# Second feed-forward entry: scaling and split by token halves, late factors tied behind direct evacuations, weight sums on VectorE

## The chip, the cores and the metric

The kernel runs on one core of a Trainium2 chip. The time is device microseconds of one execution. The engines are TensorE (PE, matmuls; PEld is its weight load), VectorE (DVE), ScalarE (ACT), GpSimd (POOL) and SyncE (SP, which issues DMAs). Each takes its instructions in a fixed order.

## What is computed

One inference step of a decoder of two layers, for a prompt of 512 tokens and a sample group of 8 tokens that share the weights. The width D is 1024, the feed-forward width 4096. Everything is float32. Cut to what matters:

```python
def rmsnorm(x, g):
    xf = x.astype(F32)
    y = xf * lax.rsqrt(jnp.mean(xf * xf, axis=-1, keepdims=True) + EPS)
    return (y * g.astype(F32)).astype(x.dtype)

def sq_relu_mlp(x, g, w_up, w_down):
    h = rmsnorm(x, g) @ w_up
    return jnp.square(jax.nn.relu(h)) @ w_down

def retention_layer(x, mem_k, mem_v, s0, g_mix, w_in, w_out, g_mlp, w_up, w_down):
    ...
    x = x + jnp.concatenate([o_ret, o_mem], axis=-1) @ w_out
    return x + sq_relu_mlp(x, g_mlp, w_up, w_down), s_new

def window_layer(x, k_ctx, v_ctx, decode, mem_k, mem_v, sinks, g_mix, w_in, w_out, g_mlp, w_up, w_down):
    ...
    x = x + jnp.concatenate([o_swa, o_mem], axis=-1) @ w_out
    return x + sq_relu_mlp(x, g_mlp, w_up, w_down)
```

The trunk is the retention layer, the window layer, and a last rmsnorm.

## The kernel before

The 512 + 8 tokens stand together as 520 columns (`TT`), features on the partitions, so the stream `x` is 8 tiles (`KT`) of 128 features x 520 tokens. `HALVES` are tokens 0 to 255 and 256 to 519, which gives products of 256 and 264 columns. Each float32 operand is split into a high and a low part: ACT casts the high part, DVE subtracts it for the low part. A product of two such operands is three matmuls for each tile: high weight with high and with low activation, low weight with high activation (`product`, L233).

The program has four phases, one after the other: A (retention layer), FA (`mlp(0, False)`, its feed-forward part), B (window layer), FB (`mlp(1, True)`). Each phase has a tile pool of its own, and the pools use the same memory in turn, so a first tile of a phase waits until the tile of the phase before that lay there was read for the last time.

**`mlp`.** The feed-forward width is cut into 4 groups of 8 blocks of 128. `up(g)` makes the 8 blocks of a group, `down(g)` multiplies them into the stream; `ORDER_F` says in which order steps of `up(g)` and `down(g-1)` follow one another, in rounds of one `up` pair and two `down` blocks. In group 0 the first four blocks are direct products, `u100` to `u103` in FB (`u000` to `u003` in FA). The other pairs of blocks go through `seven`: a product of two blocks by seven smaller ones (as in Strassen's method), for which the activations are combined into seven factors, `op[1]` to `op[7]`, and the weights into four sums (`total`, L320), whose engines the string `ENG_W` gives, by pairs of blocks in turn. A `seven` is 84 matmuls on PE (L298); its evacuations are L333 to L349, then L831 and L832.

**`operands`** makes what the entry of a feed-forward phase needs. For each of the 8 tiles, in the order 0, 4, 1, 5, 2, 6, 3, 7 (`BY_PAIR`), it scales `x` by a gain and the factor of the norm before (`f1xg`, L276), splits the result for the direct products (`direct.put`, the low part `hid` of L178), adds the squares of `x` for the norm (`norm.add`: ACT squares, L378, and DVE adds to `f1acc`, L382), and makes the factors from pairs of tiles: four combinations (L264) and seven splits (the low part is L253) for each pair, 11 DVE instructions. The direct products need only the split; the factors are needed from `u104` on.

**The norm.** `m.finish` sums `f1acc` over the partitions on PE (`f1ms`, L392), makes the inverse root by a chain of small DVE steps (L394 to L363, ending in `ry`), spreads it over the partitions (`f1mt`, L409) and copies it on ACT (`f1r`, L413). Only then can the first direct blocks be evacuated (L823). PE's banks for the products are few: three `mm`, two `ws`, two `wt`, one `ot`. Raw weights, high parts and low parts have three buffers each.

The end of phase B is its output projection: the products `ob`, of operands `obh` and `obl` that are split from `wo` (ACT L177, DVE L178), and the residuals `xs` (L440).

The source says what depends on what; the order on each engine is set by the framework's scheduler when the program is built.

Of the kernel before, what the change touches and what calls it, by code (L numbers as in the profile page):

```python
# [16 lines left out]
ALU = mybir.AluOpType  # L17
# [14 lines left out]
FFG = 4  # L32
FK = 8
DIRECT = 2
UK = KT // 2
BY_PAIR = [kt + i * UK for kt in range(UK) for i in range(2)]
EPS = 1e-6
# [7 lines left out]
ROLE_U = ('mm', 'mm', 'mm', 'ws')  # L45
ORDER_F = "uddudduddudd"
ENG_UL = "vvvvvvvv"
ENG_R = dict(a='ppppvppv', m='pppppppv', f='vvvvvvvv', b='vvvvvpvv', y='vppppppv')
ENG_B = "pvvvvvvv"
ENG_W = "pvppppvp"  # L50
BUFS_W = dict(wr=3, wh=3, wl=3)
BUFS_A = dict(blk=2, qkv=6, wp=2, mp=4, wpT=3, qw=1, kvs=1, ld=5)
BANKS = dict(mm=3, ws=2, wt=2, ot=1)
# [62 lines left out]
def build(tc, d, o):  # L116
    nc = tc.nc
    with ExitStack() as ctx:
# [20 lines left out]
        def half(name, dt=F32, shape=None):  # L139
            return hp.tile(shape or [P, 4, TT], dt, name=name, tag="half")  # L140

        def blk(name, shape=None, tag="blk", dt=F32):
            return now["w"].tile(shape or [P, TT], dt, name=name, tag=tag, bufs=now["tags"][tag])
# [11 lines left out]
        f = lambda ap: ap.bitcast(F32)  # L155
        v2 = lambda ap: ap.rearrange("p (a b) -> p a b", a=2)

        class Pair:
# [25 lines left out]
        x = [xs[:, kt, :] for kt in range(KT)]  # L184
# [14 lines left out]
        def gain(name, kt):  # L199
            return gains[:, GAINS.index(name), kt:kt + 1]  # L200
# [45 lines left out]
            nc.vector.scalar_tensor_tensor(  # L246
                out=a.lo(kt), in0=x[kt], scalar=gain(g, kt), in1=f(a.hi(kt)), op0=ALU.mult, op1=ALU.subtract)

        def cut(op, j, src, eng):

            h, l = op[:, 0, j, :], op[:, 1, j, :]
            nc.scalar.copy(out=h, in_=src)
            eng.tensor_sub(out=l, in0=src, in1=f(h))  # L253

        def operands(name, g, scale, direct, norm):

            op, first = {}, {}
            left, right = slice(0, EVEN), slice(EVEN, TT)  # L260

            def combine(i, j, x0, x1, alu):
                t = blk(f"{name}t{i}{j}", [P, EVEN], "t")
                nc.vector.tensor_tensor(out=t, in0=x0, in1=x1, op=alu)  # L264
                put(i, j, t)
                return t

            def put(i, j, src):
                if i not in op:
                    op[i] = half(f"{name}{i}", F32R, [P, 2, UK, EVEN])  # L270
                cut(op[i], j, src, nc.vector)

            for n, kt in enumerate(BY_PAIR):
                j = kt % UK
                y = blk(f"{name}xg{kt}", tag="u")
                nc.vector.scalar_tensor_tensor(out=y, in0=x[kt], scalar=gain(g, kt), in1=scale, op0=ALU.mult, op1=ALU.mult)  # L276
                direct.put(kt, y)
                norm.add(n, x[kt])
                if kt < UK:
                    first[j] = y  # L280
                    put(1, j, y[:, left])
                    combine(5, j, y[:, right], y[:, left], ALU.subtract)
                else:
                    b11, b12, b21, b22 = first[j][:, left], first[j][:, right], y[:, left], y[:, right]
                    t = combine(7, j, b22, b12, ALU.subtract)
                    t = combine(6, j, t, b11, ALU.add)
                    put(3, j, b22)
                    combine(4, j, b21, t, ALU.subtract)
                    put(2, j, b21)
            return op  # L290

        def times(t, w, op, more=False):

# [7 lines left out]
        def seven(src, op, u, name, turn):  # L301


            n = UK * P
            raw = [wp.tile([P, KT * P], F32, name=f"{name}r{i}", tag="wr", bufs=BUFS_W["wr"]) for i in range(2)]
# [62 lines left out]
        class Rms:  # L368
# [6 lines left out]
            def add(self, kt, src):  # L375
# [120 lines left out]
            yield  # L496


        def side_by_side(*pairs):


            last = None
            for pair in pairs:
                for m in reversed(pair):
                    i = m()  # L505
                    if last is not None:
                        tc.add_manual_dep(i.ins, last.ins.name, mybir.DependencyInfo(
                            mybir.DependencyClass.NoSync, mybir.DependencyReason.DATA), reason="side by side")
                    last = i

        def mem_attention(l, qm, out):
# [281 lines left out]
        def mlp(l, last):  # L793
            before, scale = now["norm"]
# [4 lines left out]
            def room(name, odd):  # L799
                t = Pair(name)  # L800
                if odd:
                    t.t.update({(part, i): high[:, 2 * j + i] for j, part in enumerate("hl") for i in range(2)})
                return t

            hids = [room(f"hid{l}{g}", g % 2) for g in range(FFG)]
            xg = room(f"xg{l}", True)
            m = Rms(TT, TT // 5, f"f{l}", "blk")
            op = operands(f"f{l}", f"mlp{l}", scale, xg, m)
            r = []

            def up(g, hid):

                n0 = 2 * DIRECT if g == 0 else 0
                for n in range(n0):
                    w = weights(d["w_up"][l, g * FK + n], D, f"u{l}{g}{n}")
                    t = [part(f"u{l}{g}{n}", s, ROLE_U[(2 * n + s) % len(ROLE_U)]) for s in range(2)]
                    for s in range(2):
                        product(t[s], w, xg, 0, s, BY_PAIR, 1, BY_PAIR)
                    if not r:
                        r.append(m.finish(before)[1])  # L820
                    u = blk(f"u{l}{g}{n}", tag="u")
                    for s, ts in enumerate(HALVES):
                        nc.vector.scalar_tensor_tensor(out=u[:, ts], in0=t[s], scalar=0.0, in1=r[0][:, ts], op0=ALU.max, op1=ALU.mult)  # L823
                    nc.scalar.square(out=u, in_=u)
                    hid.put(n, u)
                    yield
                for n in range(n0, FK, 2):
                    u = [blk(f"u{l}{g}{n}{i}", tag="u") for i in range(2)]
                    seven([d["w_up"][l, g * FK + n + i] for i in range(2)], op, u, f"u{l}{g}{n}", n // 2)
                    for i in range(2):  # L830
                        nc.vector.scalar_tensor_tensor(out=u[i], in0=u[i], scalar=0.0, in1=r[0], op0=ALU.max, op1=ALU.mult)  # L831
                        nc.scalar.square(out=u[i], in_=u[i])  # L832
                        hid.put(n + i, u[i])
                    yield
# [280 lines left out]
```

## Time and profile before

| | us |
|---|---|
| median of 3 runs | 1238.98 |
| lowest and highest | 1237.83, 1239.64 |
| profiled execution | 1237.81 |
| its span | 1236.0 |
| DVE busy | 833.5 |
| ACT busy | 534.1 |
| POOL busy | 221.3 |

The span goes from the first to the last instruction of the profiled execution; its time includes 1.8 us more around it. The mean granted clock of TensorE was 0.983 of its full speed.

### The profile page before, as it was taken

The numbers are of one execution on the slowest core, as the hardware profiler recorded it, in microseconds if no ns is written. First come the engines' busy times: TensorE is split into PE (matmuls) and PEld (weight loads), VectorE is DVE, ScalarE is ACT, GpSimd is POOL, SyncE is SP. The second block draws the span as 40 slices with busy tenths as digits, with TensorE's granted clock in tenths as the row PEclk, the third lists the DMA queues.
The fourth block names the chain that finished last, engine by engine and source line by source line (L and its number), as shares of the span: only waits on it lengthen the run. The fifth ranks groups of instructions, "written<-read, shape, count | busy, mean of one in ns | idle before, by whom it ended". The sixth has DMA issues, their size and how long they took to land. (4 is left out here: it accounts for less than half of the span.)

```text
span 1236.0 us, 23670 instructions
## 1 busy us (share of the span) xinstructions
PE 1198.1 (97%) x9718; PEld 1140.1 (92%) x9718; DVE 833.5 (67%) x1616; ACT 534.1 (43%) x997; POOL 221.3 (18%) x196
## 2 busy tenths in 40 slices
PE   8999999999999999999999998899799999999996
PEld 7999989999999999999999786579799999999996
DVE  7676777789766666675557658558786576666634
ACT  6232442354554444444324326455464444444532
POOL 2301100001312112121024114110232121121110
PEclk9999999999999999999999998889799999999998
DMA  8345622222223232232324354001122232322412
GB/s 308 108 150 174 213 77 72 88 86 72 75 94 120 86 120 87 101 103 77 122 94 143 105 165 145 27 1 54 49 100 105 77 113 86 119 87 95 142 38 69
DMA packets 43724, 128.25 MB, mean 104 GB/s; under 512 B 5048, under 2 KB 10304, under 8 KB 43488
## 3 DMA queue, kind: packets, MB, share of 16 engines
q1 hardware_dynamic: 41376, 119.79, 28.1%
q0 software_dynamic: 2240, 6.95, 1.6%
q8 instruction: 76, 1.25, 0.4%
q14 instruction: 32, 0.26, 0.1%
HBM read 117.65 MB, written 9.08 MB: 103 GB/s over the span
## 5 line engine op out<-in xcount | busy, mean ns | idle before, releaser
L440 DVE TENSOR_TENSOR xs<-d,xs 128x264 f32<-128x264 f32 (+1 forms) x128 | 53.9, 422 | 102.2 <-PE d L233 102.2
L233 PE MATMUL d<-hid,dw 128*128 128x256 f32 (+1 forms) x384 | 46.9, 283 | 0.0
L233 PEld LDWEIGHTS d<-hid,dw 128*128 128x128 f32 x384 | 46.3, 188 | 0.1
L832 ACT ACTIVATE u<-u 128x520 f32<-128x520 f32 x56 | 35.6, 636 | 21.9 <-DVE u L831 21.9
L641 POOL DMA_DIRECT2D out_ret_s<-s x12 | 6.8, 569 | 135.5 <-DVE s L640 102.8
L702 ACT ACTIVATE wp<-wp,wnm 128x256 f32<-128x256 f32 (+1 forms) x48 | 22.5, 471 | 13.3 <-DVE wes L699 9.4
L233 PE MATMUL ob<-obh,obw 128*128 128x256 f32 (+1 forms) x128 | 26.8, 297 | 0.9 <-ACT obh L177 0.7
L707 POOL TENSOR_SCALAR wp<-wp,wsm 128x256 f32<-128x256 f32 (+1 forms) x32 | 15.4, 496 | 53.7 <-ACT wp L702 27.3
L233 PEld LDWEIGHTS ob<-obh,obw 128*128 128x128 f32 x128 | 21.3, 197 | 3.3 <-ACT obh L177 1.7
L178 DVE TENSOR_TENSOR hid<-u,hid 128x520 fp32r<-128x520 f32 x32 | 23.2, 726 | 0.0
L831 DVE SCALAR_TENSOR_TENSOR u<-u,f1r 128x520 f32<-128x520 f32 x28 | 22.7, 811 | 0.4
L831 DVE SCALAR_TENSOR_TENSOR u<-u,f0r 128x520 f32<-128x520 f32 x28 | 22.7, 811 | 0.4
L526 ACT ACTIVATE p<-ms,nm 128x256 f32<-128x256 f32 x32 | 14.8, 475 | 18.5 <-DVE nm L524 16.8
L715 PEld LDWEIGHTS wt<-c,wp 128*128 128x128 f32 x84 | 10.4, 154 | 12.9 <-POOL wp L707 7.2
L715 PE MATMUL wt<-c,wp 128*128 128x128 f32 x84 | 16.4, 312 | 5.1 <-POOL wp L707 2.7
L177 ACT CAST hid<-u 128x520 fp32r<-128x520 f32 x32 | 20.1, 628 | 1.0
L233 PE MATMUL ob<-obl,obw 128*128 128x256 f32 (+1 forms) x64 | 18.4, 300 | 1.6 <-DVE obl L178 1.6
L178 DVE TENSOR_TENSOR obl<-wo,obh 128x128 fp32r<-128x128 f32 x24 | 6.9, 288 | 17.5 <-ACT obh L177 17.5
L505 PE MATMUL ws<-kvb,qb 64*128 64x256 f32 (+1 forms) x96 | 16.6, 433 | 1.3 <-DVE wp L692 0.6
L524 DVE TENSOR_REDUCE nm<-ms 128x2 f32<-128x512 f32 x16 | 10.3, 685 | 10.1 <-PE ms L505 10.1
L717 ACT COPY wpT<-wt 128x384 f32<-128x384 f32 x28 | 12.8, 479 | 8.6 <-PE wt L715 8.0
L692 DVE SCALAR_TENSOR_TENSOR wp<-cb,ws 128x256 f32<-128x256 f32 (+1 forms) x48 | 15.4, 375 | 0.1
(1996 smaller groups left out, 5115.1 us busy)
## 6 DMA issues: line engine op xcount, KB each, us to landing
kc<-in_mem_k SPq DMA_DIRECT2D x16, 256.0 KB, 4.3
vc<-in_mem_v SPq DMA_DIRECT2D x16, 256.0 KB, 4.6
s<-in_S SPq DMA_DIRECT2D x12, 256.0 KB, 5.2
out_ret_s<-s POOLq DMA_DIRECT2D x12, 256.0 KB, 2.6
xs<-in_xT SPq DMA_DIRECT2D x8, 260.0 KB, 4.3
out_yT<-xs SPq DMA_DIRECT2D x2, 528.0 KB, 3.2
memx<-in_memT SPq DMA_DIRECT2D x1, 1024.0 KB, 9.0
u004r<-in_w_up SPq DMA_DIRECT2D x2, 512.0 KB, 3.2
```

What stands on the lines that cost most here:

```text
L177: nc.scalar.copy(out=self.hi(kt, sl, rows), in_=src)
L178: eng.tensor_sub(out=self.lo(kt, sl, rows), in0=src, in1=f(self.hi(kt, sl, rows)))
L233: nc.tensor.matmul(t, w[:, ws], a(kt, HALVES[s]), start=kt == k[0] and m == 0, stop=kt == k[-1] and m == 2)
L440: nc.vector.tensor_add(out=x[mb][:, ts], in0=t, in1=x[mb][:, ts])
L505: i = m()
L526: nc.scalar.activation(out=t[:, b, :], in_=s[hh][:, b, :], func=AF.Exp, bias=nm[:, b:b + 1], accum_out=sm[:, b:b + 1])
L692: nc.vector.scalar_tensor_tensor(out=pv[:, j, :], in0=cb["nd"][:, k0:], scalar=float(SLOPES[6 * kb + j]), in1=sv[j // 3][j % 3], op0=ALU.m ...
L702: nc.scalar.activation(out=pv[:, j, :], in_=pv[:, j, :], func=AF.Exp, bias=nm[:, j:j + 1], accum_out=sm[:, j:j + 1])
L707: (nc.gpsimd if j % 3 in POOL_N else nc.vector).tensor_scalar(out=pv[:, j, :], in0=pv[:, j, :], scalar1=sm[:, j:j + 1], scalar2=1.0, op0=A ...
L715: nc.tensor.transpose(t[:, i * P:i * P + P], p[:, 3 * hh + i, kk * P:kk * P + P], ident)
L831: nc.vector.scalar_tensor_tensor(out=u[i], in0=u[i], scalar=0.0, in1=r[0], op0=ALU.max, op1=ALU.mult)
L832: nc.scalar.square(out=u[i], in_=u[i])
```

## The change

There are four parts.

- Late factors: the factors of the first two pairs of tiles are made at once, those of the last two (`LATE = 2`) only in `up(0)`, behind the first and the second direct block. Each DVE instruction of these is tied by an order dependence (`behind`) to come after the block's second evacuation; the casts on ACT aren't tied. This holds for both feed-forward phases.
- Halves: in FB alone, the scaling and the split for the direct products are done for tokens 0 to 255 and for 256 to 519 apart.
- Weight sums: all four sums of each `seven` are on DVE. In the program 84 of them were on POOL.
- The sums of squares of the last norm (`y`): six that were on POOL are on DVE.

```diff
+LATE = 2
...
-ENG_R = dict(a='ppppvppv', m='pppppppv', f='vvvvvvvv', b='vvvvvpvv', y='vppppppv')
+ENG_R = dict(a='ppppvppv', m='pppppppv', f='vvvvvvvv', b='vvvvvpvv', y='vvvvvvvv')
 ENG_B = "pvvvvvvv"
-ENG_W = "pvppppvp"
+ENG_W = "vvvvvvvv"
...
-        def operands(name, g, scale, direct, norm):
-            op, first = {}, {}
+        def operands(name, g, scale, direct, norm, parts):
+            op, order = {}, {}
             left, right = slice(0, EVEN), slice(EVEN, TT)
+
+            def follow(i):
+                if order["follow"]:
+                    behind(i, order["follow"])
 
             def combine(i, j, x0, x1, alu):
                 t = blk(f"{name}t{i}{j}", [P, EVEN], "t")
-                nc.vector.tensor_tensor(out=t, in0=x0, in1=x1, op=alu)
+                follow(nc.vector.tensor_tensor(out=t, in0=x0, in1=x1, op=alu))
                 put(i, j, t)
                 return t
...
-                cut(op[i], j, src, nc.vector)
+                follow(cut(op[i], j, src))
+
+            def factors(j, upper, lower, follow=None):
+                b11, b12, b21, b22 = (t[:, c] for t in (upper, lower) for c in (left, right))
+                order["follow"] = follow
+                put(1, j, b11)
+                combine(5, j, b12, b11, ALU.subtract)
+                t = combine(7, j, b22, b12, ALU.subtract)
+                t = combine(6, j, t, b11, ALU.add)
+                put(3, j, b22)
+                combine(4, j, b21, t, ALU.subtract)
+                put(2, j, b21)
+
+            later = []
             for n, kt in enumerate(BY_PAIR):
-                j = kt % UK
                 y = blk(f"{name}xg{kt}", tag="u")
-                nc.vector.scalar_tensor_tensor(out=y, in0=x[kt], scalar=gain(g, kt), in1=scale, op0=ALU.mult, op1=ALU.mult)
-                direct.put(kt, y)
+                for ts in parts:
+                    nc.vector.scalar_tensor_tensor(out=y[:, ts], in0=x[kt][:, ts], scalar=gain(g, kt), in1=scale[:, ts],
+                                                   op0=ALU.mult, op1=ALU.mult)
+                    direct.put(kt, y[:, ts], ts)
                 norm.add(n, x[kt])
...
-            return op
+                later.append(y)
+                if n < KT - 2 * LATE and n % 2:
+                    factors(n // 2, *later)
+                    later = []
+            return op, lambda i, follow: factors(UK - LATE + i, *later[2 * i:2 * i + 2], follow)
...
+        def behind(i, first):
+
+            tc.add_manual_dep(i.ins, first.ins.name, mybir.DependencyInfo(
+                mybir.DependencyClass.NoSync, mybir.DependencyReason.DATA), reason="order")
...
-            op = operands(f"f{l}", f"mlp{l}", scale, xg, m)
+            op, late = operands(f"f{l}", f"mlp{l}", scale, xg, m, HALVES if last else [slice(0, TT)])
...
-                        nc.vector.scalar_tensor_tensor(out=u[:, ts], in0=t[s], scalar=0.0, in1=r[0][:, ts], op0=ALU.max, op1=ALU.mult)
+                        i = nc.vector.scalar_tensor_tensor(out=u[:, ts], in0=t[s], scalar=0.0, in1=r[0][:, ts], op0=ALU.max, op1=ALU.mult)
                     nc.scalar.square(out=u, in_=u)
                     hid.put(n, u)
+                    if n < LATE:
+                        late(n, i)
                     yield
```

How the order on DVE moves is shown at three places. Numbers behind the names tell tiles apart. The lines are those of each kernel's own file: L276 of before is L294 of after, L178 is L179, L253 is L254, L264 is L270, L320 is L332, L382 is L394, L440 is L452, L823 is L839.

The first place is the end of phase B and the beginning of FB, where `obl` is the low part of an operand of the output projection, split from the last product `wo13`, and `hid1` the low part of the scaled input. Before:

```order
L178 TENSOR_TENSOR obl0_8829<-wo13_9759,obh0_8827 128x128
L178 TENSOR_TENSOR obl1_8157<-wo13_9759,obh1_8155 128x128 x2
L440 TENSOR_TENSOR xs_75<-ob01_9866,xs_75 128x264
L440 TENSOR_TENSOR xs_75<-ob41_9892,xs_75 128x264
L440 TENSOR_TENSOR xs_75<-ob11_9918,xs_75 128x264
L276 SCALAR_TENSOR_TENSOR f1xg0_10112<-xs_75,gains_73,br_7968 128x520
L276 SCALAR_TENSOR_TENSOR f1xg4_10125<-xs_75,gains_73,br_7968 128x520
```

After, from the same place on:

```order
L294 SCALAR_TENSOR_TENSOR f1xg0_10112<-xs_75,gains_73,br_7968 128x256
L294 SCALAR_TENSOR_TENSOR f1xg4_10120<-xs_75,gains_73,br_7968 128x256
L294 SCALAR_TENSOR_TENSOR f1xg1_10159<-xs_75,gains_73,br_7968 128x256
L294 SCALAR_TENSOR_TENSOR f1xg5_10169<-xs_75,gains_73,br_7968 128x256
L294 SCALAR_TENSOR_TENSOR f1xg2_10201<-xs_75,gains_73,br_7968 128x256
L179 TENSOR_TENSOR obl0_8829<-wo13_9759,obh0_8827 128x128
L179 TENSOR_TENSOR hid1_10110<-f1xg0_10112,hid1_10110 128x256
L179 TENSOR_TENSOR hid1_10110<-f1xg4_10120,hid1_10110 128x256
L179 TENSOR_TENSOR hid1_10110<-f1xg1_10159,hid1_10110 128x256
L179 TENSOR_TENSOR hid1_10110<-f1xg5_10169,hid1_10110 128x256
L179 TENSOR_TENSOR hid1_10110<-f1xg2_10201,hid1_10110 128x256
L179 TENSOR_TENSOR obl1_8157<-wo13_9759,obh1_8155 128x128 x2
```

Five scalings of the first half, and their low parts, now stand among the splits of `wo13`; the residuals and the other scalings follow.

The second place is the end of the entry of FB on DVE, up to the last square sum. Before:

```order
L320 TENSOR_TENSOR u104s0_10556<-u104s0_10556,u104r0_10549 128x512
L178 TENSOR_TENSOR hid1_10110<-f1xg7_10238,hid1_10110 128x520
L253 TENSOR_TENSOR f13_10142<-f1xg7_10238,f13_10142 128x260
L253 TENSOR_TENSOR f12_10150<-f1xg7_10238,f12_10150 128x260
L264 TENSOR_TENSOR f1t42_10219<-f1xg6_10202,f1t62_10213 128x260
L264 TENSOR_TENSOR f1t53_10234<-f1xg3_10225 128x260
L382 TENSOR_TENSOR f1acc_10111<-f1acc_10111,f1sq7_10242 128x520
```

After:

```order
L179 TENSOR_TENSOR hid1_10110<-f1xg7_10231,hid1_10110 128x256
L394 TENSOR_TENSOR f1acc_10111<-f1acc_10111,f1sq6_10228 128x520
L332 TENSOR_TENSOR u104s0_10580<-u104r1_10574 128x512
L332 TENSOR_TENSOR u104s1_10581<-u104r0_10573,u104r1_10574 128x512
L179 TENSOR_TENSOR hid1_10110<-f1xg7_10231,hid1_10110 128x264
L332 TENSOR_TENSOR u104s0_10580<-u104s0_10580,u104r0_10573 128x512
L394 TENSOR_TENSOR f1acc_10111<-f1acc_10111,f1sq7_10238 128x520
L332 TENSOR_TENSOR u104s1_10581<-u104r0_10573,u104s0_10580 128x512
```

The factors of the third and fourth pair of tiles are gone from this place, and three weight sums of `u104` stand ahead of the last square sum instead of one.

The third place is DVE behind the chain of the norm, whose last step is `ry`. Before:

```order
L363 SCALAR_TENSOR_TENSOR ry5_10324<-rqt_10331,rqu_10330 104x5
L823 SCALAR_TENSOR_TENSOR u100_10353<-u1000_10267,f1r_10343 128x256
L823 SCALAR_TENSOR_TENSOR u101_10417<-u1010_10367,f1r_10343 128x256
L823 SCALAR_TENSOR_TENSOR u100_10353<-u1001_10268,f1r_10343 128x264
L823 SCALAR_TENSOR_TENSOR u101_10417<-u1011_10368,f1r_10343 128x264
L178 TENSOR_TENSOR hid10l0_10359<-u100_10353,hid10h0_10357 128x520
```

After:

```order
L375 SCALAR_TENSOR_TENSOR ry5_10304<-rqt_10311,rqu_10310 104x5
L839 SCALAR_TENSOR_TENSOR u100_10333<-u1000_10247,f1r_10323 128x256
L839 SCALAR_TENSOR_TENSOR u100_10333<-u1001_10248,f1r_10323 128x264
L254 TENSOR_TENSOR f11_10130<-f1xg2_10201,f11_10130 128x260
L270 TENSOR_TENSOR f1t52_10343<-f1xg2_10201 128x260
L270 TENSOR_TENSOR f1t72_10347<-f1xg6_10211,f1xg2_10201 128x260
L254 TENSOR_TENSOR f13_10148<-f1xg6_10211,f13_10148 128x260
L254 TENSOR_TENSOR f12_10156<-f1xg6_10211,f12_10156 128x260
L270 TENSOR_TENSOR f1t62_10351<-f1t72_10347,f1xg2_10201 128x260
L254 TENSOR_TENSOR f15_10135<-f1t52_10343,f15_10135 128x260
L179 TENSOR_TENSOR hid10l0_10339<-u100_10333,hid10h0_10337 128x520
```

The late factors of the third pair stand directly behind the two evacuations of `u100`, and those of `u101` come after them.

## Rows read from the trace of the kernel before

**Rows 1.** The page's list of engines: busy us, share of the span, instructions.

```profile
PE 1198.1 (97%) x9718; PEld 1140.1 (92%) x9718; DVE 833.5 (67%) x1616; ACT 534.1 (43%) x997; POOL 221.3 (18%) x196
```

**Rows 2.** PE's waits, 840 to 920: us in total, times, longest.

```profile
PE u L233 <- DVE hid L178: 5.0, 2, 3.0
PE u L233 <- DVE u L823: 1.0, 1, 1.0
PE u110a L298 <- DVE u110l L315: 0.9, 1, 0.9
```

**Rows 3.** Windows: length, busy PE PEld DVE ACT POOL, granted clock, DMA, GB/s.

```profile
340.00:350.00 10.00, 9.06 (x75) 8.95 (x75) 8.32 (x12) 8.14 (x14) 0.00 (x0) 1.00 0.34 125
840.00:860.00 20.00, 20.00 (x167) 19.92 (x166) 20.00 (x41) 14.77 (x30) 0.00 (x0) 1.00 0.17 58
860.00:880.00 20.00, 14.87 (x90) 13.73 (x89) 18.84 (x37) 9.08 (x19) 7.17 (x3) 0.72 0.13 49
880.00:900.00 20.00, 17.66 (x137) 17.24 (x137) 14.04 (x34) 8.85 (x17) 5.00 (x3) 0.94 0.15 53
...
920.00:1160.00 240.00, 239.86 (x1997) 239.66 (x1996) 155.66 (x201) 107.43 (x160) 46.74 (x33) 1.00 0.28 97
```

**Rows 4.** Windows of 1 us for PE alone: length, busy, granted clock, DMA, GB/s.

```profile
867.00:868.00 1.00, 0.00 (x0) 1.00 0.00 0
...
869.00:870.00 1.00, 1.00 (x7) 0.50 0.00 0
```

**Rows 5.** DVE's timeline in FB: start, us, engine, line, out<-in, idle before.

```profile
839.09 1.11 DVE L440 TENSOR_TENSOR xs<-ob,xs 128x264 f32<-128x264 f32 x3 [1.88 <-PE ob L233]
...
856.89 0.75 DVE L276 SCALAR_TENSOR_TENSOR f1xg<-xs,gains,br 128x520 f32<-128x520 f32 x1
857.56 1.21 DVE L215 TENSOR_TENSOR u101l<-u101r,u101h 128x1024 fp32r<-128x1024 f32 x1
858.69 0.42 DVE L253 TENSOR_TENSOR f<-f1t,f 128x260 fp32r<-128x260 f32 x1
...
859.37 0.68 DVE L382 TENSOR_TENSOR f1acc<-f1acc,f1sq 128x520 f32<-128x520 f32 x1
...
871.84 1.73 DVE L320 TENSOR_TENSOR u104s<-u104s,u104r 128x512 f32<-128x512 f32 x1 [1.16 <-POOL u104s L320]
873.49 0.69 DVE L178 TENSOR_TENSOR hid<-f1xg,hid 128x520 fp32r<-128x520 f32 x1
874.10 1.84 DVE L253 TENSOR_TENSOR f<-f1xg,f 128x260 fp32r<-128x260 f32 x2
...
876.54 0.69 DVE L382 TENSOR_TENSOR f1acc<-f1acc,f1sq 128x520 f32<-128x520 f32 x1
...
884.61 0.17 DVE L363 SCALAR_TENSOR_TENSOR ry<-rqt,rqu 104x5 f32<-104x5 f32 x1
885.99 1.43 DVE L823 SCALAR_TENSOR_TENSOR u<-u,f1r 128x256 f32<-128x256 f32 x4 [1.21 <-ACT f1r L413]
...
910.21 0.68 DVE L320 TENSOR_TENSOR u110s<-u110s,u110r 128x512 f32<-128x512 f32 x1
```

**Rows 6.** The timeline of ACT and of DVE at the end of phase B.

```profile
835.38 0.27 ACT L177 CAST obh<-wo 128x128 fp32r<-128x128 f32 x1 [2.65 <-PE wo L505]
835.67 0.29 DVE L178 TENSOR_TENSOR obl<-wo,obh 128x128 fp32r<-128x128 f32 x1 [2.63 <-ACT obh L177]
```

**Rows 7.** PE's timeline from the first direct block of FB to the first `seven`.

```profile
857.02 0.41 PE L233 MATMUL u<-hid,u101h 128*128 128x264 f32 x2
...
877.28 1.89 PE L392 MATMUL f1ms<-c,f1acc 128*104 128x1 f32 x10
...
886.47 0.51 PE L233 MATMUL u<-hid,u102h 128*128 128x256 f32 x2 [0.98 <-DVE u L823]
...
895.19 0.40 PE L298 MATMUL u104a<-f,u104h 128*128 128x260 f32 x2
```

**Rows 8.** ACT's timeline: the cast of the weights of `u103`.

```profile
875.29 1.06 ACT L214 CAST u103h<-u103r 128x1024 fp32r<-128x1024 f32 x1 [4.85 <-PE u L233]
```

**Rows 9.** PE's waits in FA, 300 to 350: us in total, times, longest.

```profile
PE u010a L298 <- DVE u010l L315: 0.9, 1, 0.9
```

More of the change, by code (lines that the diff above doesn't have):

```diff
@@ L247, in split, with cut @@
                 out=a.lo(kt), in0=x[kt], scalar=gain(g, kt), in1=f(a.hi(kt)), op0=ALU.mult, op1=ALU.subtract)
-        def cut(op, j, src, eng):
+        def cut(op, j, src):
             h, l = op[:, 0, j, :], op[:, 1, j, :]
             nc.scalar.copy(out=h, in_=src)
-            eng.tensor_sub(out=l, in0=src, in1=f(h))
-        def operands(name, g, scale, direct, norm):
-            op, first = {}, {}
+            return nc.vector.tensor_sub(out=l, in0=src, in1=f(h))
+        def operands(name, g, scale, direct, norm, parts):
+            op, order = {}, {}
             left, right = slice(0, EVEN), slice(EVEN, TT)
+            def follow(i):
+                if order["follow"]:
+                    behind(i, order["follow"])
             def combine(i, j, x0, x1, alu):
                 t = blk(f"{name}t{i}{j}", [P, EVEN], "t")
-                nc.vector.tensor_tensor(out=t, in0=x0, in1=x1, op=alu)
+                follow(nc.vector.tensor_tensor(out=t, in0=x0, in1=x1, op=alu))
                 put(i, j, t)
@@ L270, in put @@
                     op[i] = half(f"{name}{i}", F32R, [P, 2, UK, EVEN])
-                cut(op[i], j, src, nc.vector)
+                follow(cut(op[i], j, src))
[10 more added lines that the diff above has]
+            later = []
             for n, kt in enumerate(BY_PAIR):
-                j = kt % UK
                 y = blk(f"{name}xg{kt}", tag="u")
-                nc.vector.scalar_tensor_tensor(out=y, in0=x[kt], scalar=gain(g, kt), in1=scale, op0=ALU.mult, op1=ALU.mult)
-                direct.put(kt, y)
+                for ts in parts:
+                    nc.vector.scalar_tensor_tensor(out=y[:, ts], in0=x[kt][:, ts], scalar=gain(g, kt), in1=scale[:, ts],
+                                                   op0=ALU.mult, op1=ALU.mult)
+                    direct.put(kt, y[:, ts], ts)
                 norm.add(n, x[kt])
[L279 to L289, printed above, removed]
-            return op
+                later.append(y)
[3 more added lines that the diff above has]
+            return op, lambda i, follow: factors(UK - LATE + i, *later[2 * i:2 * i + 2], follow)
         def times(t, w, op, more=False):
@@ L506, in side_by_side @@
                     if last is not None:
-                        tc.add_manual_dep(i.ins, last.ins.name, mybir.DependencyInfo(
-                            mybir.DependencyClass.NoSync, mybir.DependencyReason.DATA), reason="side by side")
+                        behind(i, last)
                     last = i
```

## Prediction

> **What bounds the kernel now.** I began with the page's list of engines [rows 1]: TensorE (PE) is busy for 1198.1 us of the span of 1236.0, so what a change of this size can win lies in PE's waits and in the clock that PE was granted. VectorE (DVE) is busy for 833.5 us, two thirds, which says little, since it is an average over stages. I therefore read PE's waits in the stretch from the end of phase B into the second feed-forward layer, FB [rows 2]: two waits, 5.0 us together, for `hid` of L178, the low part of the scaled input, which DVE makes; then 1.0 us for the first evacuations (L823), and 0.9 us at `u110`. Next the windows of that stretch [rows 3]. From 840 to 860 DVE is busy for 20.00 of 20 us and PE too; from 860 to 880 DVE still for 18.84, while PE falls to 14.87 and the granted clock to 0.72. So DVE sets the entry of FB. In the long rounds, 920 to 1160, PE is busy for 239.86 of 240 us and DVE for 155.66: there PE sets it.
>
> The clock by single microseconds [rows 4]: PE does nothing from 867 to 868, at 1.00, and in the stretch that follows the clock is at 0.50, which is 1.2 of 2.4 GHz. From the two means, 0.72 and 0.94, I work out how long: 0.28 x 2 x 20 + 0.06 x 2 x 20 = 13.6 us. So lateness on DVE is paid twice here, as PE's wait and as the slow level after it.
>
> DVE's row of work [rows 5] begins at 839.09, with the residual of phase B's last product, and goes to 876.54, the last sum of squares (`f1acc`). A DVE instruction begins 0.08 us before its forerunner ends (856.89 + 0.75 against 857.56), so I count a row's duration less 0.08: 0.67 for a scaling of 520 columns, 0.60 for an addition or subtraction of 520, 1.13 for 1024 columns, 0.34 for 256 to 264, 0.60 for a weight sum of 512 that nothing disturbs (910.21). Between the anchors stand 71 instructions in DVE's order: 8 scalings, 8 low parts, 4 weight splits, 35 instructions of the factors, 1 weight sum, 6 square sums, 9 residuals. 8 x 0.67 + 8 x 0.60 + 4 x 1.13 + 35 x 0.34 + 0.60 + 6 x 0.60 + 9 x 0.34 = 33.9 us. It took 37.45. The rest is GpSimd (POOL): DVE waits 1.16 us for POOL's first sum of `u104`, its own sum beside POOL's takes 1.73 in place of 0.68, and the pair at 874.10 takes 1.84 in place of 0.34 + 0.42.
>
> **The change, part by part.** *The entry of FB.* After the change 66 instructions stand between the same anchors: 11 half scalings and 11 half low parts (five of each are already done, below), 4 weight splits, 22 of the factors instead of 35, 3 weight sums, 6 square sums, 9 residuals: 11 x 0.34 + 11 x 0.34 + 4 x 1.13 + 22 x 0.34 + 3 x 0.60 + 6 x 0.60 + 9 x 0.34 = 28.0 us, with no POOL beside them. That is 9.4 us less than 37.45. The halves themselves cost: 0.68 for two against 0.67 or 0.60 for one whole, 8 x 0.01 + 8 x 0.08 = 0.7 us, already in the sum.
>
> The Trainium skill, Perfetto Trace Analysis, section Optimizing Scalar/DVE Operations, speaks against the halving: larger operations are better on an engine that is full, since each DVE instruction has some 60 ns of its own on SBUF. By it 16 more instructions would cost an estimated 1.0 us rather than 0.7, and the gain would be 0.3 us smaller.
>
> *What the halves do ahead of the anchor.* In the new order five first-half scalings stand on DVE ahead of the low part (`obl`) of phase B's last `wo` product, and their low parts between that and the next two. They can't be early: in the program the first of them waits for the same last matmul of `wo13` that ScalarE's (ACT's) cast waits for, because FB's memory is phase B's; that cast starts at 835.38 [rows 6]. So five scalings, 5 x 0.34 = 1.7 us, come first and the `obl` of 835.67 moves to about 837.1; five casts and five low parts stand ahead of the next. PE, which in the old order takes these operands almost as they come, waits some 1.0 us for the first and 0.85 for the second: 1.85 us in all. At best this is 0 (DVE is idle for 2.63 us ahead of 835.67, if the wait ends sooner than I think). The anchor moves to 840.94 and the last square sum to 840.94 + 28.0 = 868.9, 7.6 us before the old 876.54.
>
> *PE from there.* A matmul takes 239.86/1997 = 0.120 us at the full level [rows 3]. In the old order PE begins on `u101` at 857.02 [rows 7]; in the new one at 857.02 + 1.85 = 858.9, with no wait for `hid`, since the low parts now come with their scalings and 13 factor instructions are out of their way. Blocks `u100` and `u101`, 96 matmuls, end at 870.4. The sums over partitions (`f1ms`, 1.89 us at the low level for 10 matmuls, so about 0.9 at the full one) have their input by then. `u103`'s weights are cast when `u100` frees their buffer (the cast takes 1.06 [rows 8]) and split by DVE (1.13): at 872.4. DVE does one weight split of `u104` and the chain of twelve small steps at 0.2 us (0.17 busy and a gap of 0.03): `ry` at 876.1. From `ry` to the first evacuation was 1.21 us, and from that to `u102` 0.48 (885.99 to 886.47): `u102` at 877.8 instead of 886.47, 8.7 us earlier. PE is idle some 3 us in three pieces on the way. As a check: 857.02 to 895.19 holds 192 matmuls, 22.9 us, and some 1.5 of small ones, so 13.8 us are lost there now; of these 3.2 and 1.85 stay, and 13.8 - 5.05 = 8.7.
>
> *The late factors.* From `u102` to the first `seven` (895.19) takes 8.72 us, PE's own work. The 22 instructions that were put off, 22 x 0.34 = 7.5 us, now stand there beside 8 evacuations and 4 low parts. The second pair's last factors run into `u104`, ready by my count within 0.1 us of PE's need. In `u104` to `u110` DVE has 4 x 0.60 of sums, 3 x 1.13 + 0.60 of splits, 3 x 0.34 of additions, 2 x 0.67 and 2 x 0.60 behind them, 10.0 us, against 84 x 0.120 = 10.1 of PE. I take 0.5 us of waits in place of the 0.9 at `u110`: 0.4 gained; at worst 1.5 in each of three (the largest single wait for DVE that rows 2 show at a product is 3.0; this is half of it).
>
> *The first feed-forward layer* (FA) has no halves. PE's list there has the same 1.0 us for L823 and 0.9 for `u010l` [rows 9]. The second goes, since the factors no longer stand ahead of it; a smaller `f0` list brings the chain forward by some 0.3: 1.2 us, at least 0.
>
> *Weight sums on DVE, 84 of them.* In rounds without late factors a pair of `up` blocks is followed by two `down` blocks: PE 180 matmuls, 21.6 us; DVE 10.0 + 2 x (1.13 + 0.68) = 13.6. Even all 33 POOL instructions of 920 to 1160 at 0.60 make DVE 155.66 + 19.8 = 175.5 of 240. I cost it at nothing, with PE as cover; without cover three sums more in a `seven` are 1.8 us. The six square sums of `y0` move to a DVE that is idle in the tail: nothing.
>
> The sum: 8.7 + 0.4 + 1.2 = 10.3 us from the profiled execution, 1237.81 (1236.0 of span and 1.8 around it): 1227.5. That execution lies 1.2 us below the median of 1238.98; on the median it is 1228.7, and I say 1228.5. Its own range is 1226 (no wait at `wo13`) to 1231 (nothing in FA, 1.3 us more in the sevens).
>
> **The rivals.** *The clock falls in the new gaps.* It fell behind 2 us of an idle PE [rows 4]. The forecast has a gap of up to 1.85 us at `wo13` and three of about 1 us from 870 to 878. Against it: the 0.9 us of FA lie in a window at 1.00 [rows 3, 9]. If it falls for 4 to 14 us (the last is the old stretch), 2 to 7 us are lost: about 1233.
>
> *DVE is full behind the late factors.* At 10.0 against 10.1 us, `u104` to `u110` have no slack; each order that isn't perfect becomes a wait. 1.5 us in each of three: 1233. The same section of the skill would have work taken off a full DVE, to GpSimd if need be, and so speaks for this rival; the 1.73 us of a sum beside POOL [rows 5] speak against that remedy here.
>
> *The other side: sums hold up DVE's queue.* POOL could wait for a weight block's landing without holding anyone. On DVE a sum that waits stands ahead of evacuations and residuals, and with three `mm` banks PE soon waits too. 28 `seven`s have three more sums each. It decides from 10.3/28 = 0.37 us each; with 0.6, about one sum that isn't covered, 16.8 us are lost: 1245. Against it: DVE's 155.66 of 240.
>
> *No wait at `wo13`*, and a smoother end of phase B: 1.85 and up to 1.5 of the gaps: 1225. *It does nothing*, because something else ends the entry just as late: 1239; the 5.0 us for `hid` speak against that.
>
> **How the numbers follow.** The forecast 0.53, clock 0.16, a full DVE 0.10, no wait at `wo13` 0.07, sums in the queue 0.10, nothing 0.04. 1223 to 1236 takes in nearly all of the first four but their tails, 0.80. Less than 0.2%, 2.5 us, can't be told from no change. The first four are faster (0.86, less 0.02 for tails), 0.06 no change, 0.10 slower.
>
> **What would show it.** Right: no wait for `hid` between 857 and 872, a wait for `obl` of 1 to 2 us at about 836, `u102` at 877 to 879, `u104` at 885.5 to 887.5, a clock of 1.00 from 860 on, POOL without a sum, 920 to 1160 as full on PE as before. Wrong: a clock of 0.5 for more than 3 us behind 836; waits of over 1 us each at `u104` to `u110`; waits for sums (now L332) or for evacuations in the rounds.

## The result, and the profile after

The changed kernel takes 1226.82 us (median of 4 runs, 1226.4 to 1228.01), the kernel before 1238.4 beside it: a ratio of 0.9905, 95% interval 0.9894 to 0.9917, so 11.6 us less. The profiled execution has a span of 1224.9 us, 11.1 less than the 1236.0 before.

PE's waits of the changed kernel from 820 to 910, to set against [rows 2] (us in total, times, longest):

```profile
PE wt L731 <- ACT wpT L733: 1.8, 1, 1.8
PE ob L234 <- DVE obl L179: 1.7, 2, 1.2
PE u L234 <- DVE u L839: 1.0, 1, 1.0
PE u L234 <- DVE u103l L216: 0.7, 1, 0.7
PE u106a L310 <- DVE u106l L327: 0.4, 1, 0.4
```

The 5.0 us for `hid` are gone, and the 0.9 at `u110`. The 1.7 for `obl` are new, in two pieces, and so are 0.7 for the weights of `u103` and 0.4 at `u106`. The windows, in the columns of [rows 3]:

```profile
840.00:860.00 20.00, 20.00 (x169) 20.00 (x168) 20.00 (x49) 14.29 (x34) 0.00 (x0) 1.00 0.23 79
860.00:870.00 10.00, 9.32 (x79) 8.97 (x78) 9.71 (x20) 5.21 (x10) 0.00 (x0) 1.00 0.16 55
870.00:880.00 10.00, 9.02 (x61) 8.82 (x62) 7.66 (x26) 3.15 (x8) 0.00 (x0) 0.83 0.31 106
...
920.00:1150.00 230.00, 230.00 (x1917) 230.00 (x1916) 152.28 (x222) 100.74 (x150) 0.00 (x0) 1.00 0.28 95
```

POOL does nothing in these stretches any more. In the long rounds PE is busy for all of the 230 us, so the sums cost nothing there. The clock's mean is 0.83 in one window of 10 us: 0.17 x 2 x 10 = 3.4 us at the lower level in place of 13.6. DVE's timeline of the entry, which answers to [rows 5]:

```profile
832.43 2.07 DVE L294 SCALAR_TENSOR_TENSOR f1xg<-xs,gains,br 128x256 f32<-128x256 f32 x5 [2.40 <-PE wo L522]
834.41 0.29 DVE L179 TENSOR_TENSOR obl<-wo,obh 128x128 fp32r<-128x128 f32 x1
...
838.27 0.77 DVE L452 TENSOR_TENSOR xs<-ob,xs 128x264 f32<-128x264 f32 x2 [1.07 <-PE ob L234]
838.96 0.48 DVE L294 SCALAR_TENSOR_TENSOR f1xg<-xs,gains,br 128x264 f32<-128x264 f32 x1
839.36 0.43 DVE L452 TENSOR_TENSOR xs<-ob,xs 128x264 f32<-128x264 f32 x1
...
865.53 0.68 DVE L332 TENSOR_TENSOR u104s<-u104r,u104r 128x512 f32<-128x512 f32 x1
...
867.08 0.69 DVE L394 TENSOR_TENSOR f1acc<-f1acc,f1sq 128x520 f32<-128x520 f32 x1
...
873.22 0.17 DVE L375 SCALAR_TENSOR_TENSOR ry<-rqt,rqu 104x5 f32<-104x5 f32 x1
875.35 0.76 DVE L839 SCALAR_TENSOR_TENSOR u<-u,f1r 128x256 f32<-128x256 f32 x2 [1.97 <-ACT f1r L425]
```

The five scalings stand ahead of `obl` and wait for the last `wo` matmul, as the order said; the last square sum comes 28.81 us behind the first residual (37.45 before). PE, to set against [rows 7]:

```profile
867.83 1.08 PE L404 MATMUL f1ms<-c,f1acc 128*104 128x1 f32 x10
...
869.93 0.39 PE L234 MATMUL u<-hid,u103l 128*128 128x264 f32 x1 [0.68 <-DVE u103l L216]
...
874.24 0.61 PE L421 MATMUL f1mt<-c,ry 104*128 104x104 f32 x5
875.83 0.50 PE L234 MATMUL u<-hid,u102h 128*128 128x256 f32 x2 [0.98 <-DVE u L839]
...
884.55 0.28 PE L310 MATMUL u104c<-f,u104h 128*128 128x260 f32 x1
```

`u104` now begins with part c, at 884.55: 8.72 us behind `u102`, as before.

**Where the time came from.** I cut each execution at five places in PE's and ACT's timeline: the first matmul of `oa` (the output projection of phase A), of `u012a`, of `kv` (behind FA), the cast of `wo13` (end of phase B), and the first matmul of `u112a`. In us, and for the last two columns the time at the lower clock level, worked out as above from windows of 1 us. The starts are read to tenths, so each length is good to 0.1; the stretches ahead of `oa` and from `u012a` to `kv` are left out. The rows e1 to e11 are the experiments described below:

| kernel | oa to u012a (FA's entry) | kv to wo13 (phase B) | wo13 to u112a (FB's entry) | u112a to the end | low clock, 640 to 834 | low clock, 834 to 900 |
|---|---|---|---|---|---|---|
| before | 113.2 | 176.0 | 99.8 | 300.8 | 20.5 | 13.7 |
| after | 111.7 | 174.5 | 92.1 | 300.4 | 6.8 | 3.4 |
| e1 without halves | 111.7 | 174.6 | 91.6 | 300.1 | 10.2 | 3.4 |
| e2 without late factors | 113.1 | 175.2 | 98.9 | 300.1 | 10.2 | 13.7 |
| e3 without sums on DVE | 114.1 | 176.9 | 96.0 | 300.8 | 17.1 | 3.4 |
| e4 scalings behind obl | 111.7 | 174.0 | 91.9 | 300.1 | 10.2 | 3.4 |
| e5 sums alone | 114.6 | 175.8 | 98.7 | 300.1 | 10.2 | 17.1 |
| e6 late factors alone | 114.1 | 176.2 | 96.2 | 300.4 | 10.2 | 6.8 |
| e7 halves alone | 113.4 | 175.6 | 100.3 | 300.6 | 13.6 | 10.2 |
| e8 after, with 12 matmuls | 111.7 | 174.3 | 91.0 | 300.4 | 3.4 | 0.0 |
| e9 before again | 113.4 | 175.6 | 101.5 | 300.3 | 13.6 | 13.7 |
| e10 after again | 111.7 | 177.1 | 92.9 | 300.1 | 13.7 | 3.4 |
| e11 e4 and e8 together | 111.7 | 173.4 | 94.8 | 300.2 | 13.6 | 6.8 |

From before to after: 1.5 in FA, 1.5 in phase B, 7.7 in FB's entry, 0.4 behind it: 11.1 us. PE's waits in FA from 300 to 350, before and after:

```profile
PE u L233 <- DVE u L823: 1.0, 1, 1.0
PE u010a L298 <- DVE u010l L315: 0.9, 1, 0.9
PE u L233 <- DVE u003l L215: 0.2, 1, 0.2
```

```profile
PE u006a L310 <- DVE u006l L327: 0.4, 1, 0.4
PE u L234 <- DVE u L839: 0.3, 1, 0.3
```

### The profile page after: what moved, and what is told of

It is laid out like the page before. It is cut to its first block, busy times and chain, and to the rows that moved or that the text cites. A ratio compares the mean times of both kernels' runs of the same rounds, so it can differ in the third digit from the quotient of the medians.

```text
span 1224.9 us, 23596 instructions
## 1 busy us (share of the span) xinstructions
PE 1191.3 (97%) x9718; PEld 1134.2 (93%) x9718; DVE 840.1 (69%) x1722; ACT 533.1 (44%) x1005; POOL 91.5 (7%) x106
## 4 chain that ended last, share of the span: by engine, by line
PE 85%; DVE 8%; ACT 2%; issue 2%; DMA 1%; POOL 0%; SPq 0%; DVEq 0%; POOLq 0%
PE d L234 28%; PE qkv L234 9%; PE oa L234 4%; PE qb L234 3%; PE ga L234 3%; PE u L234 2%; PE ob L234 2%; PE kv L234 2%; ACT wp L718 1%; PE ms L522 1%; PE memv L502 1%; PE memk L491 1%; DVE f L254 1%; DVE wp L708 1%; PE mt L554 1%
## 5 line engine op out<-in xcount | busy, mean ns | idle before, releaser
L452 DVE TENSOR_TENSOR xs<-d,xs 128x264 f32<-128x264 f32 (+1 forms) x128 | 54.3, 425 | 115.6 <-PE d L234 115.6
L179 POOL TENSOR_TENSOR bl<-xs,bh 128x520 fp32r<-128x520 f32 x1 | 1.8, 1812 | 371.9 <-ACT bh L178 371.9
L234 PEld LDWEIGHTS ob<-obh,obw 128*128 128x128 f32 x128 | 20.5, 188 | 4.2 <-ACT obh L178 2.0
L179 DVE TENSOR_TENSOR hid<-u,hid 128x520 fp32r<-128x520 f32 x32 | 22.2, 693 | 0.0
L178 ACT CAST hid<-u 128x520 fp32r<-128x520 f32 x32 | 20.1, 628 | 1.0
L849 DVE SCALAR_TENSOR_TENSOR u<-u,f1r 128x520 f32<-128x520 f32 x28 | 19.5, 696 | 0.4
L849 DVE SCALAR_TENSOR_TENSOR u<-u,f0r 128x520 f32<-128x520 f32 x28 | 19.5, 696 | 0.4
L540 DVE TENSOR_REDUCE nm<-ms 128x2 f32<-128x512 f32 x16 | 10.3, 685 | 11.8 <-PE ms L522 11.8
L234 PEld LDWEIGHTS ob<-obl,obw 128*128 128x128 f32 x64 | 12.1, 188 | 4.7 <-DVE obl L179 3.6
L179 DVE TENSOR_TENSOR obl<-wo,obh 128x128 fp32r<-128x128 f32 x24 | 6.9, 289 | 13.1 <-ACT obh L178 13.0
```

The lines of the kernel that those rows point to most:

```text
L234: nc.tensor.matmul(t, w[:, ws], a(kt, HALVES[s]), start=kt == k[0] and m == 0, stop=kt == k[-1] and m == 2)
L452: nc.vector.tensor_add(out=x[mb][:, ts], in0=t, in1=x[mb][:, ts])
```

## The experiments

My theory, A: DVE's row of work sets both entries, and the gain is what the late factors and the missing POOL take from it; the wait at `wo13` is a price without effect on the end. Rivals: the halves make a good part of it (B); the work is only moved; the clock alone does it. The times come with the interval of their ratio; against the change they can tell a difference of some 2 us and no less, so smaller ones are read from the traces, most of which are of a single execution.

**e1, without the halves.**

```diff
-            op, late = operands(f"f{l}", f"mlp{l}", scale, xg, m, HALVES if last else [slice(0, TT)])
+            op, late = operands(f"f{l}", f"mlp{l}", scale, xg, m, [slice(0, TT)])
```

Expected: 

> The changed kernel with the scaling and the split of the second feed-forward layer whole again (520 columns); late factors and weight sums stay as changed. Theory A (DVE's count sets the entry, and PE's wait of 1.7 us for obl at wo13 is the price of the halves): DVE then has 59 instructions, 30.0 us, between the first residual and the last square sum instead of 66 and 28.6, but the residual comes 1.7 us sooner because nothing stands ahead of obl. The last square sum comes 1.0 us sooner counted from wo13's cast (34.7 us now); the time is 0 to 1.5 us shorter, about 1226. Theory B (the halves make a good part of the gain, since low parts come in the order in which PE takes them): waits for hid come back and the time is 2 to 4 us longer, about 1230.

Measured: 1228.76 us, ratio 0.9914 (0.9901 to 0.9927), which can't be told from the change's 0.9905. The wait for `obl` is gone and 1.4 us for `hid` are there; FB's entry takes 91.6 us against 92.1. By the two ratios e1 lies between 1 us ahead of the change and 3 behind it, so the time alone doesn't exclude the lower end of B, and the waits for `hid` that B named did come back. But the last square sum comes 33.96 us behind `wo13`'s cast instead of 34.72, as A said, and `u104` 0.6 us sooner: the traces, and e7 below, show no gain by the halves.

**e2, without the late factors**, and **e3, without the sums on DVE.**

```diff
-LATE = 2
+LATE = 0
```

```diff
-ENG_W = "vvvvvvvv"
+ENG_W = "pvppppvp"
```

Expected of e2: 

> The changed kernel with LATE = 0: all factors at once, as before; halves and sums stay as changed. Theory A (the factors' 13 to 15 instructions on DVE are what held up the entry): 81 instructions, 33.7 us, in place of 28.6, so the last square sum is 5 us later; PE waits for hid as before, and the clock falls in those waits: 5 to 8 us longer, about 1233. Rival (the work is only moved, and DVE has to do it before u104 either way): at most 1.5 us longer.

Measured: 1236.95 us, ratio 0.9984 (0.9975 to 0.9993), some 10 us slower than the change: more than A said. The last square sum comes 39.73 us behind `wo13`'s cast instead of 34.72, the 5 us that A named; 2.2 us for `hid` come back, and 13.7 us at the lower level. FB's entry loses 6.8 us and FA's, which A left out, 1.4.

Expected of e3: 

> The changed kernel with the old engines for the weight sums (POOL has 84 of them again); late factors and halves stay. Theory A (POOL costs DVE 3.4 us at the entry: a wait for a sum, and instructions slowed beside POOL): the last square sum comes about 2 us later, u104 too, 2 to 4 us longer in all, about 1230; the long rounds are unchanged. Rival (DVE is full in u104 to u110, so sums on POOL help there): the same or up to 1.5 us shorter.

Measured: 1235.24 us, ratio 0.9968 (0.9956 to 0.9979), some 8 us slower, twice what A said, and the rival has the wrong sign. FB's entry loses 3.9 us, FA's 2.4; there the time is longer than before the change (114.1 against 113.2). The last square sum comes only 1.2 us later (35.94 behind the cast); the rest is lost at the `seven`s, where PE waits 1.5 us at `u106`, 0.9 at `u110` and 0.4 at `u104` in FB, and nearly the same in FA (1.4, 0.9, 0.4). By the ratios, taking out the late factors costs five sixths of the gain and taking out the sums two thirds: they aren't two terms of a sum.

**e4, the scalings tied behind the last `obl`.** `now["wo13"]` is the last low part that is split from `wo13`.

```diff
...
+                    if len(parts) > 1:
+                        behind(i, now["wo13"])
...
```

Expected: 

> The changed kernel with the scalings tied behind the last obl of wo13, so nothing of the second feed-forward layer stands ahead of it on DVE. Theory A (DVE sets the entry): PE's two waits for obl (1.7 us) go, but the last square sum comes at the same time as now within 0.4 us, since DVE does the same work and only fills its idle time less well; the time is the same within 0.8 us, and PE idles later instead. Theory B (a wait of PE there is lost time): 1.7 us shorter, about 1225.

Measured: 1227.9 us, ratio 0.9908 (0.9895 to 0.992): no change. In its trace PE's wait for `obl` is gone, and 0.8 (for `xs`), 0.7 (for `hid`) and 0.5 us (for `f1acc`) stand in its place; the last square sum comes 34.78 us behind `wo13`'s cast, against 34.72, since DVE has the same work to do. `u104` begins 0.6 us sooner, of which 0.2 are left at `u112a`. So PE's wait of 1.7 us at `wo13` costs next to nothing.

**e5, sums alone; e6, late factors alone; e7, halves alone.** Each is one part of the change on the kernel before (the diff ahead of the prediction, cut to that part). They keep the rewritten `operands`, though, which writes the factors of a pair behind its second tile, where the kernel before began with those of the first tile as soon as it was scaled; no run has this alone.

Expected of e5: 

> The kernel before with one edit: all weight sums on DVE (no late factors, no halves, the sums of squares of the last norm as before). Theory S (the parts need one another: with the factors still in the entry, the three sums of u104 only lengthen DVE's row there, 71 instructions of 34.4 us, and what goes is POOL's disturbance of 3.4 us): 2 to 3.5 us shorter, about 1236. Rival (the first four runs were spoiled by the halves' wait at wo13; without it the sums alone are worth more): 5 us or more shorter. The other rival, sums holding up DVE's queue in the long rounds: no shorter, PE waits in 920 to 1150.

Expected of e6: 

> The kernel before with one edit: the late factors (no halves, weight sums and sums of squares as before). DVE's row in the entry falls from 71 to 58 instructions, 33.8 to 29.4 us, but POOL still disturbs it and makes the sums of u104 to u110 late. Theory S: 3 to 5 us shorter, about 1235, with waits of about 1 us each at u106 and u110 of both feed-forward layers. Rival (late factors alone make the gain): 8 us or more shorter.

Expected of e7: 

> The kernel before with one edit: the halves (all factors early, weight sums and sums of squares as before). Theory A (the wait of 1.7 us for obl at wo13 buys five scalings and five low parts, 3.4 us, but eight splits cost 0.7 more): the last square sum is 0 to 1 us later; the time is the same within 1 us. Rival (halves bring the operands sooner): 2 us or more shorter.

Measured: e5 1236.93 us, ratio 0.9977 (0.9966 to 0.9989); e6 1234.4 us, 0.9965 (0.9954 to 0.9977); e7 1239.29 us, 1.0002 (0.9992 to 1.0012). The first two gain 0.23% and 0.35%, 0.58% together, against 0.86% for both in one kernel (e1; by the three intervals the difference is 0.28% give or take 0.21) and 0.95% for the change. In e5 PE still waits for `hid`, 3.4 us. In e6 this wait is 0.3 us, but PE waits 2.3 us for `f1acc`, and elsewhere behind that. PE's waits of e6 from 895 to 925, and DVE's timeline there:

```profile
PE u106a L310 <- DVE u106l L327: 1.5, 1, 1.5
PE u110a L310 <- DVE u110l L327: 0.9, 1, 0.9
PE u104a L310 <- DVE f L254: 0.4, 1, 0.4
```

```profile
901.37 1.22 DVE L327 TENSOR_TENSOR u106l<-u106r,u106h 128x1024 fp32r<-128x1024 f32 x1
...
906.38 2.32 DVE L327 TENSOR_TENSOR u106l<-u106s,u106h 128x1024 fp32r<-128x1024 f32 x1
908.62 0.68 DVE L332 TENSOR_TENSOR u110s<-u110s,u110r 128x512 f32<-128x512 f32 x1
909.22 1.77 DVE L327 TENSOR_TENSOR u106l<-u106r,u106h 128x512 fp32r<-128x512 f32 x1
910.91 1.77 DVE L849 SCALAR_TENSOR_TENSOR u<-u,f1r 128x520 f32<-128x520 f32 x1
...
914.69 0.69 DVE L849 SCALAR_TENSOR_TENSOR u<-u,f1r 128x520 f32<-128x520 f32 x1
```

POOL's timeline in the same stretch:

```profile
906.00 1.60 POOL L332 TENSOR_TENSOR u110s<-u110r 128x512 f32<-128x512 f32 x1 [7.61 <-DMA u110r<-in_w_up]
908.77 1.67 POOL L332 TENSOR_TENSOR u110s<-u110r,u110r 128x512 f32<-128x512 f32 x1 [1.17 <-DVE u106l L327]
910.40 1.73 POOL L332 TENSOR_TENSOR u110s<-u110r,u110s 128x512 f32<-128x512 f32 x1
```

The same split of 1024 columns takes 1.22 us alone and 2.32 beside a sum on POOL; the three slowed instructions lose about 3.3 us (2.32, 1.77 and 1.77, less 1.22 for the like alone, 0.68 for one of 512 columns as at 908.62, and 0.69 for one of 520 as at 914.69), just where the late factors have filled DVE. The Trainium skill, SBUF — State Buffer, section Who interferes with whom, says that a DVE instruction with two SBUF inputs and a GpSimd instruction that reads SBUF hold each other up; these rows agree, and POOL's sums take 1.60 to 1.73 us here against 1.28 at 928.27, where DVE stands idle.

So late factors need POOL out of the way. Alone they bring `u104` to 53.68 us behind `wo13`'s cast (59.81 before, 51.60 in e1), but from there to `u112a` it takes 42.5 us instead of 40.0, and FA's entry gets 0.9 longer: with late factors and POOL's sums together PE waits 2.8 us at the `seven`s of each layer, against 0.9 before and 0.4 in after. The sums alone win little, since without late factors no more than those 0.9 us are to be won there. Of e5's two entries one must be read with care: in FA 3.4 us lie at the lower clock level, which no other run has there. e2, in which FA is the same program, doesn't have them, and its FA takes 113.1 us against 114.6. The window from 310 to 320 for PE, e5 and then e2:

```profile
310.00:320.00 10.00, 7.80 (x52) 0.83 0.14 52
```

```profile
310.00:320.00 10.00, 7.81 (x65) 1.00 0.15 52
```

**e8, after with 12 more matmuls behind `f1ms`**, ahead of `u103`. They write to a bank that nobody reads.

```diff
...
+                if fill is not None:
+                    z = ps(f"{name}fill", "wt")
+                    for _ in range(FILL):
+                        behind(nc.tensor.matmul(z[:, 0:EVEN], fill.hi(0, slice(0, P)), fill.hi(0, slice(0, EVEN)), start=True, stop=True), i_ms)
...
```

Expected: 

> The changed kernel with 12 more matmuls of 128x128 by 260 columns on PE, behind the sums over partitions (f1ms) of the second feed-forward layer and ahead of u103; their result isn't read. They take 1.44 us, 0.7 of it in what is now PE's wait for u103l. If PE's idle 0.7 us behind the small matmuls is what lets the granted clock fall to 0.5 for 3.3 us there, the clock stays at 1.00, the first half of u103 ends about 1 us sooner, f1mt no longer waits for PE, and u102 comes 0.5 to 0.9 us sooner: 0 to 1 us shorter. If the clock falls for another reason, it falls as now and the time is 0.5 to 0.8 us longer.

Measured: 1227.37 us, ratio 0.9903 (0.9888 to 0.9918), no difference to the change that the timing can tell. The trace shows it. PE by single microseconds (length, busy, granted clock, DMA, GB/s), first of after, then of e8:

```profile
869.00:870.00 1.00, 0.32 (x3) 1.00 0.00 0
870.00:871.00 1.00, 1.00 (x7) 0.75 0.30 37
871.00:872.00 1.00, 1.00 (x6) 0.50 0.84 279
```

```profile
870.00:871.00 1.00, 1.00 (x10) 1.00 0.00 0
871.00:872.00 1.00, 1.00 (x10) 1.00 0.04 12
872.00:873.00 1.00, 1.00 (x10) 1.00 0.85 299
```

With the 12 matmuls the clock stays at 1.00, and `u102` comes 42.66 us behind `wo13`'s cast instead of 43.47: the 0.8 us expected. So in these traces the fall of the clock in after follows from PE's idle time behind the small matmuls, and it costs 0.8 us.

**e9 and e10, the kernels before and after once more; e11, e4 and e8 together.**

Expected of e9: 

> The kernel before once more, for its trace. The stretch from the first matmul of kv (behind the first feed-forward layer) to the cast of wo13 took 176.0 us in the first trace of before and 174.5 in that of after, with 20.5 and 6.8 us at the lower clock level. If that difference is the clock's, which falls at other places in each execution, the stretch and its share at the lower level differ here from 176.0 and 20.5, anywhere between 174 and 177. If the change's order causes it, 176.0 within 0.3 comes again.

Expected of e10: 

> The changed kernel once more, for its trace. If the clock's fall in phase B differs from execution to execution, the stretch from kv to wo13's cast takes another time than 174.5 us and another share at the lower level than 6.8 us. If the change's order causes it, 174.5 within 0.3 comes again. From wo13's cast to the first matmul of u104 the same 52.2 us as in the first trace, within 0.3.

Expected of e11: 

> The changed kernel with both edits that shortened the stretch from wo13's cast to u104: the scalings tied behind wo13's obl (51.6 us instead of 52.2) and the 12 matmuls that keep the clock up (51.4). If the two add up, 50.8, and the time is about 1.4 us shorter than after, about 1225.5; if DVE's row sets the end whichever way, 51.4 and 0.8 us.

Measured: phase B of the changed kernel took 177.1 us this time against 174.5, with 13.7 us at the lower level against 6.8; before 175.6 against 176.0, with 13.6 against 20.5. So phase B's time differs between executions of one kernel by more than the 1.5 us that it gave in the first pair. Up to the first matmul of `u104` it was 52.21 us from `wo13`'s cast in e10, against 52.19 in the first trace of after. In e9 `u104` comes 61.39 us behind the cast, against 59.81, although `u102` comes at 51.14, against 51.09: the 1.5 us are lost on PE between `u102` and `u104`, where e9 has the lower clock level (0.51 in the window from 888 to 891) and the first trace of before doesn't (1.00 from 887 to 896). e2 and e5 have it there too, and the same 10.2 us instead of 8.7. e11 took 1227.5 us, ratio 0.99 (0.9884 to 0.9917); a gain of 1.4 us would be within that. Its trace is of the slowest of its four executions (1230.38 us), and in that one the two edits don't add up. With the scalings tied back, PE's idle time lies ahead of `f1ms` (busy 0.14 of the microsecond from 867), where no matmuls fill it; the lower level lasts 6.8 us, `u104` comes 54.60 us behind the cast, and FB's entry takes 94.8 us. No version was measurably faster than the change.

## Why the prediction was right

1228.5 us were forecast, 1226.82 measured, and the terms hold in the main. They come to 0.7 us less than their sum, though (the last point of this list), so that the median is 1.7 us better than forecast isn't their merit; phase B alone differs by more than that between executions.

- **FB's entry** was to be 8.7 us shorter up to the first `seven`. Counted from `wo13`'s cast to the first matmul of `u104`, 59.81 (835.38 to 895.19) has become 52.19 (832.36 to 884.55): 7.6. The wait at `wo13` was to be 1.85 and is 1.7. DVE's row was to be 28.0 us and is 28.81: a half scaling takes 0.40 (838.96 to 839.36), not the 0.34 of a subtraction of that size, and 11 x 0.06 = 0.7. But that isn't what is missing: counted from the cast, the last square sum comes 1.2 us later than forecast (34.72 against 33.5), and `ry` only 0.1 (40.86 against 40.72). The other 0.9 are lost between `ry` and the first evacuation, which took 1.38 us before (884.61 to 885.99; the forecast's 1.21 is DVE's idle time alone) and take 2.13 now (873.22 to 875.35). There the rival with the clock came true in small: 3.4 us at the lower level, so that PE was late with `f1mt`. In e8, without them, it is 1.38 again. Two of the prediction's own signs thus went against it: the clock wasn't at 1.00 from 860 on, and was at 0.50 for more than 3 us.
- The halves cost 8 x (0.80 - 0.67) + 8 x (0.68 - 0.60) = 1.7 us of DVE, not 0.7. The Trainium skill's Perfetto Trace Analysis, in Optimizing Scalar/DVE Operations, gave an estimated 1.0; the trace is above both. Its advice against small operations fits in so far as e7 shows no gain. It shows no loss in the time either: the halves bring five scalings and low parts forward into DVE's idle time ahead of the first residual, and e7's last square sum comes 41.93 us behind `wo13`'s cast, against 41.17 before.
- **Late factors** hidden behind `u102` and `u103`: right. PE waits 0.4 us at `u106` and not at all at `u110`; 0.5 were forecast. The rival of a full DVE came about only where POOL disturbs it (e3, e6).
- **FA**'s entry was to gain 1.2 and gains 1.5: the 0.9 at `u010` go, as forecast, the 1.0 for the evacuations become 0.3 and the 0.2 for `u003` go, and 0.4 at `u006` are new. But this was put down to the late factors alone, and e6 shows that these alone make FA 0.9 us longer. The sums alone change nothing that counts there (113.1 in e2; e5's 114.6 are the clock). It takes both.
- **The sums in the rounds** cost nothing: PE is full from 920 to 1150.
- The clock alone didn't do it: e5 spends more time at the lower level in FB's entry than before (17.1 against 13.7 us) and is faster, and in e8, where that time is gone, only 0.8 us more are won. Of the 7.6 us up to `u104`, 6.4 are there at the last square sum already (34.72 us behind the cast against 41.17). From the first residual to that sum DVE stands idle 1.16 us before, for POOL, and never after, so it waits for PE in neither, and PE's clock has no part in the 8.6 us by which this row is shorter. Only in the 1.2 us that come behind it can the 10 us less at the lower level have a part.
- **Phase B** wasn't in the sum. Its 1.5 us in the first pair of traces are no part of the change by e9 and e10. Between the second traces, 1237.7 and 1228.1, the difference is 9.6 us, phase B going the other way by 1.5. Without phase B, and without the 1.5 us of the clock in e9, both pairs give 9.6 us, against 10.3 in the forecast's sum.

The prediction didn't price the parts one by one, but its sum (13 factor instructions, POOL's 3.4 us, 0.9 at `u110`) reads as if they could be added. They can't: 0.58% singly, 0.86% together. That e2 and e3 cost 10 and 8 us where 5 to 8 and 2 to 4 were expected is the same error: the expectations priced FB's entry alone, and left out FA and what POOL costs at the `seven`s beside late factors.

Left open: the six sums of squares of `y` were not tried alone; the tail from `y1mt` to the end takes 7.9 us in both kernels (1228.1 to 1236.0, 1217.0 to 1224.9). The clock's fall moves FB's entry by 1.5 us between executions of one kernel (e9), so differences of that size in this column decide nothing.

## What to carry to other kernels

Where an engine is full for 35 us ahead of the bottleneck, count its instructions between two anchors, price each by start-to-start distances, and look for the work that isn't needed yet; what is moved must land where nothing slows that engine. A wait that the edit adds on PE is hardly a loss as long as the other engine sets the end: doing away with the 1.7 us at `wo13` won 0.2 in its trace (e4). Test the parts of an edit both alone and left out, since two that free the same engine may be worth more together than singly. And look at the clock of a stretch before its time is put down to an edit.

## What I had not expected of the hardware

An idle time of PE of 0.68 us behind ten tiny matmuls was followed by 3.4 us at 1.2 GHz, while 0.98 us at 874.85 in the same trace, and 0.9 in FA of before [rows 3, 9], were not. And phase B of one kernel, unchanged, spent 20.5 and 13.6 us at the lower level in two executions, that of the other 6.8 and 13.7, and its time differed by 0.4 and 2.6 us. The level alone doesn't set that time: e11 has 13.6 us at it and the shortest phase B of all, 173.4. A difference of that size between single traces says nothing about an edit.
